# A grouped 3x3 convolution: one ring of twelve places for images and results, and a loop for the first eight images on TensorE

## The chip, the cores and the metric

The kernel runs on one core of a Trainium2 chip. A core has five engines that run their own instruction streams and meet at semaphores: TensorE (PE, matmuls; PEld is its weight load), VectorE (DVE), ScalarE (ACT), GpSimd (POOL) and SyncE (SP). Sixteen DMA engines move data between the memory of the chip (HBM) and the core's on-chip memory (SBUF). Matmul results land in PSUM, from where an engine has to copy them to SBUF before a DMA can store them. The metric is the time on the device in microseconds, the median over runs.

## What is computed

Sixteen images of 64 channels, 64 by 64, are convolved with a 3x3 kernel in 8 groups, with one row and column of zero padding; the result has 128 channels.

```python
batch, c_in, h, w, c_out, k, groups = 16, 64, 64, 64, 128, 3, 8
...
x_pad = np.pad(x, ((0, 0), (0, 0), (pad, pad), (pad, pad)), mode='constant')
for g in range(groups):
    for b in range(batch):
        for co in range(c_out_per_group):
            for ci in range(c_in_per_group):
                for kh in range(k):
                    for kw in range(k):
                        output[b, g * c_out_per_group + co] += \
                            weight[g * c_out_per_group + co, ci, kh, kw] * \
                            x_pad[b, g * c_in_per_group + ci, kh:kh+h, kw:kw+w]
```

Input and output are fp32. An image is 1 MB in HBM, a result 2 MB.

## The kernel before

**Layout.** `xx` holds NX = 8 images in bf16. For each image it has four quadrants of 32 partitions, of which three are used: the middle kernel row lies in the first quadrant (the image as loaded, 32 channels on the partitions, the two halves of the 64 channels side by side), the other two quadrants hold copies of it shifted by one row up and down. So a contraction over 96 partitions covers 32 channels times the three kernel rows, and the three kernel columns are three matmuls that add up in PSUM, on views of the image shifted by a column. `ob` is a list of NOB = 4 result buffers of 2 MB, `ps` two PSUM buffers, each for half an image (32 rows).

**The steps of an image n.** POOL issues its load, with a cast from fp32 to bf16 on the way (`load`, L133). VectorE makes the two shifted copies (`shifted`, L206, copies on L211), zero rows at the edges having been written once for all eight places at the start (L146). TensorE does each half image in 24 matmuls, for 3 kernel columns, 4 stripes of 8 rows and 2 halves of the channels, the two halves next to each other in the array (`matmuls`, L252, matmuls on L271). ScalarE copies each half from PSUM to the result buffer (`evacuate`, L284, copy on L291). SP issues the store (L298); image 0 is stored in two halves, and the store of the last image is issued at the very end (L63).

**What sets the order.** There is no scheduler: each engine's instructions stand in the order in which they are written, and `Order.wait` and `Order.done` put in the semaphores by hand. TensorE waits for the shifted copies (`ready`) and for the PSUM half being free (`free`, ScalarE's semaphore). ScalarE waits for the matmuls and, from image 4 on, for the store of image n-4 that used the same buffer (L286). The load of image n+8 waits on POOL for the matmuls of image n, which used the same place (L317). Before the last store is issued, all engines come to a barrier, and POOL clears the semaphores (L321).

**The start.** The first 36 rows of images 0 and 1 come in by one plain fp32 DMA on ScalarE's queue into the last result buffer (`raw`, L122), and are cast by ScalarE and VectorE (`cast`, L220); only the rest of these two images is loaded by POOL. The weights are loaded on SP's queue, spread out by VectorE (L189), transposed by TensorE (L196) and masked (L229). A small store of 64 KB to the result of the last image goes out early (L128); the first real store waits for it (`s_warm`). `spin` (L173) keeps TensorE busy with matmuls on zeros until the first image is ready, and `IDLE` puts in waits that pass at once on VectorE and ScalarE (L151).

Of the kernel before, what the change touches and what calls it, by code (L numbers as in the profile page):

```python
# [8 lines left out]
BF16 = mybir.dt.bfloat16  # L9
ALU = mybir.AluOpType  # L10

NX = 8
NOB = 4
KQ = (1, 0, 2)
ROWS = 36
SPINS = 11, 4, 4, 3, 3
IDLE = dict(ACT=90, DVE=40)


@with_exitstack  # L20
def kernel(
    ctx: ExitStack,
    tc: tile.TileContext,
    x: bass.AP,
    weight: bass.AP,
    groups: int,
    out: bass.AP,
):
    nc = tc.nc

    B, C, H, W = x.shape
    CO, CIg, K, _ = weight.shape
# [30 lines left out]
    last = nc.sync.dma_start(out[B - 1].rearrange("co h w -> co (h w)"), t["ob"][(B - 1) % NOB])  # L63
    tc.add_manual_dep(
        last.ins, section.name,
        mybir.DependencyInfo(mybir.DependencyClass.NoSync, mybir.DependencyReason.DATA), reason="order",
    )


class Order:  # L70
# [22 lines left out]
        return self.sem, self.n  # L93


def program(nc, x, weight, out, xx, ob, w_sb, wb, mask4, mask, ident, zero, wt, ps):
    H = W = 64
    HW, CIg, COg, R, NB = H * W, 8, 16, 8, 16
    sems = []
# [33 lines left out]
    def load(n):  # L133
        s, r0 = sem(f"ld{n}"), ROWS if n < 2 else 0
        nc.gpsimd.dma_start(  # L135
            xx[QC, n % NX, :, r0:, :].rearrange("c s h w -> c s (h w)"),
            x[n].rearrange("(s c) h w -> c s h w", s=2)[:, :, r0:, :].rearrange("c s h w -> c s (h w)"),
        ).then_inc(s, 16)
        landed[n] = (s, 16)
# [4 lines left out]
    edge = []  # L144
    for kh, row in ((0, 0), (2, H - 1)):
        e = DVE.done(nc.vector.memset(xx[quad(kh), :, :, row, :], 0.0))  # L146
# [22 lines left out]
    for n in range(2, NX):  # L169
# [31 lines left out]
    spin(2, (s_raw, 16))  # L201


    ready = {}

    def shifted(n, a, b, halves=slice(0, 2)):  # L206
# [28 lines left out]
    spin(3, w_ready)  # L235

    DVE.wait(d)
    spin(4, shifted(0, 0, 32, slice(1, 2)))
    DVE.wait(a)
    ready[0, 0] = shifted(0, 0, 32, slice(0, 1))  # L240
    for half in range(2):
        a = cast(ACT, nc.scalar.copy, 1, half)
    raw_read = [a, d]


    pe = nc.tensor
    stored = [nc.alloc_semaphore(f"st{i}") for i in range(NOB)]
    uses = [0] * NOB
    free = {0: w_ready}
    wrote = {}  # L250

    def matmuls(n, s):  # L252
        u = n % NX
        for kw in (1, 0, 2):
            w0, w1 = max(0, kw - 1), min(W, W + kw - 1)
            v0 = w0 - (kw - 1)
            ws = []
            for half in range(2):
                ws.append(wt[0:96, kw, 64 * half : 64 * half + 64])
            PE.wait(w_ready, e, ready[n, s])  # L260
            for c in range(4):
                if kw == 1 and c == 0:
                    PE.wait(free.get(s))
                for half in range(2):
                    pos = dict(tile_position=(0, 64 * half))
                    r0 = 32 * s + R * c
                    x_ap = xx[0:96, u, half, r0 : r0 + R, w0:w1]
                    o_ap = ps[s][:, 512 * c : 512 * c + 512].rearrange(
                        "p (h w) -> p h w", w=W
                    )[64 * half : 64 * half + 64, :, v0 : v0 + w1 - w0]  # L270
                    ins = pe.add_instruction(  # L271
                        mybir.InstMatmult(
                            name=nc.get_next_instruction_name(),
                            engine=mybir.EngineType.PE,
                            start_tensor_calc=kw == 1, stop_tensor_calc=kw == 2,
                            tile_size=(128, 64), ldweights=c == 0, **pos,
                            ins=[pe.lower_ap(x_ap, opt=False),
                                 pe.lower_ap(ws[half], opt=False, for_matmul_weights=True)],
                            outs=[pe.lower_ap(o_ap)],
                        )  # L280
                    )
        wrote[n, s] = PE.done(ins)

    def evacuate(n, s):  # L284
        slot = n % NOB
        if n >= NOB:  # L286
            ACT.wait((stored[slot], 16 * uses[slot]))
        elif n == NOB - 1:
            ACT.wait((s_warm, 16), *raw_read)
        ACT.wait(wrote[n, s])  # L290
        free[s] = ACT.done(nc.scalar.copy(ob[slot][:, 2048 * s : 2048 * s + 2048], ps[s]))  # L291
        if s == 1 or n == 0:
            o0 = 0 if n > 0 or s == 0 else HW // 2
            o1 = HW // 2 * (s + 1)
            SP.wait(free[s], (s_warm, 16))
            if n == NB - 1:
                return
            nc.sync.dma_start(outf[n][:, o0:o1], ob[slot][:, o0:o1]).then_inc(stored[slot], 16)  # L298
            uses[slot] += 1

    for n in range(NB):
        if n == 1:
            DVE.wait(raw_read[0])
            ready[n, 0] = shifted(n, 0, 32)
        DVE.wait(landed[n])
        if n < 2:
            ready[n, 1] = shifted(n, 32, 64)
        elif n == 2:
            ready[n, 0] = shifted(n, 0, 32)
            ready[n, 1] = shifted(n, 32, 64)  # L310
        else:
            ready[n, 0] = ready[n, 1] = shifted(n, 0, H)
        for s in range(2):
            matmuls(n, s)
# [8 lines left out]
    return [(stored[n % NOB], 16 * uses[n % NOB]) for n in range(NB, NB + NOB)]  # L323
# [1 line left out]
_INS = ['x', 'weight', 'groups']  # L325
_OUTS = [((16, 128, 64, 64), 'float32')]
# [30 lines left out]
```

## Time and profile before

| | us |
|---|---|
| median of 7 runs | 125.34 |
| lowest and highest | 125.18, 126.91 |
| the profiled execution, its own time | 126.12 |
| its span | 124.4 |
| PE, DVE, ACT, POOL busy in the span | 98.0, 77.3, 67.0, 15.4 |
| HBM read and written | 16.81 MB, 33.62 MB |
| one copy of a half image on ACT | 1.87 |
| one shifted copy of a whole image on DVE (two for each image) | 2.25 |
| first image matmul starts, last PSUM copy ends | 13.88, 111.12 |
| last store issued | 111.83 |

The profile is one execution of the program on the chip. Engine times are the time that its instructions ran; an engine that waits for a semaphore is idle. The DMA share is the mean busy share of the sixteen DMA engines; since the packets of an engine overlap a little at their ends, it can come out slightly above 1. Loads are counted by the bytes that they write, in bf16, which are half of those that they read, so a time with many loads shows fewer GB/s for the same busy engines. On the side of the instructions, "PEldq", "SPq" and the like name instructions that the engine's sequencer handles by itself: waits, branches, DMA issues.

The page's groups of the work on the images, with the number of instructions, then busy time and the mean of one in ns, then the idle time of the engine before them and what ended it:

```
L271 PE MATMUL ps<-xx,wt 96*64 96x504 bf16 (+1 forms) x768 | 88.7, 394 | 6.6 <-ACT ob L291 5.7
L291 ACT COPY ob<-ps 128x2048 f32<-128x2048 f32 x32 | 59.4, 1868 | 36.0 <-PE ps L271 21.0
L211 DVE COPY xx<-xx 32x8064 bf16<-32x8064 bf16 (+4 forms) x40 | 73.3, 1832 | 0.9
L135 POOL DMA_DIRECT2D xx<-in_x_dram x16 | 14.6, 914 | 49.0 <-PE ps L271 47.9
```

A matmul takes 394 ns from its start to its modelled end, but two run side by side and follow each other closely, so 768 of them fill 88.7 us.

### The profile page before, as it was taken

To read this page: it belongs to the slowest core of one execution; us is meant where nothing else is said; L and a number is where in the kernel's file an instruction comes from. 1 tells how busy PE (TensorE), PEld (TensorE's weight loads), DVE (VectorE), ACT (ScalarE), POOL (GpSimd) and SP (SyncE) were. 2 spreads that over 40 slices of the span, in tenths; PEclk is the share of its full clock that TensorE was granted. 3 is DMA by queue.
4 is the path that set the end of the run, shared out by engine and by line. 5 is a ranking of instruction groups with operands and counts; after the bars stand their busy time and mean duration, and the time that the engine had idled before them with its cause. 6 is when DMAs were issued, how large, how long until landed. Compare 5 with 4: busy or idle time off the path is not lost.

```text
span 124.4 us, 1320 instructions
## 1 busy us (share of the span) xinstructions
PE 98.0 (79%) x796; PEld 16.2 (13%) x220; DVE 77.3 (62%) x51; ACT 67.0 (54%) x36; POOL 15.4 (12%) x23
## 2 busy tenths in 40 slices
PE   5909999996999999569998984999999999910000
PEld 1203211110111111011010100111111111100000
DVE  4039999999999999999999999993000000000000
ACT  0049965777377665280565619077766777660000
POOL 5910001032030106310060000000000000000000
PEclk9995999999999999955899998599999999985555
DMA  4999999999999999999999999999999999999991
GB/s 63 340 225 206 213 215 208 261 292 329 335 313 382 319 348 316 361 335 316 332 429 414 313 385 432 432 432 427 437 427 421 427 437 432 432 427 432 437 395 58
DMA packets 4166, 42.72 MB, mean 343 GB/s; under 512 B 704, under 2 KB 832, under 8 KB 960
## 3 DMA queue, kind: packets, MB, share of 16 engines
q1 hardware_dynamic: 2736, 33.66, 64.2%
q0 software_dynamic: 1280, 7.80, 30.5%
q10 hardware_dynamic: 144, 1.18, 3.1%
q8 instruction: 4, 0.07, 0.2%
q14 instruction: 2, 0.02, 0.0%
HBM read 16.81 MB, written 33.62 MB: 405 GB/s over the span
## 4 chain that ended last, share of the span: by engine, by line
PE 39%; DMA 27%; DVE 17%; ACT 5%; issue 1%; SPq 0%
PE ps L271 39%; DMA out_dram<-ob 21%; DVE xx L211 16%; DMA w_sb<-in_weight_dram 6%; ACT ob L291 5%; DVE xx L220 1%; DVE wt L229 0%; DVE wb L189 0%; SPq L352 0%; SPq L50 0%
## 5 line engine op out<-in xcount | busy, mean ns | idle before, releaser
L271 PE MATMUL ps<-xx,wt 96*64 96x504 bf16 (+1 forms) x768 | 88.7, 394 | 6.6 <-ACT ob L291 5.7
L291 ACT COPY ob<-ps 128x2048 f32<-128x2048 f32 x32 | 59.4, 1868 | 36.0 <-PE ps L271 21.0
L211 DVE COPY xx<-xx 32x8064 bf16<-32x8064 bf16 (+4 forms) x40 | 73.3, 1832 | 0.9
L271 PEld LDWEIGHTS ps<-xx,wt 96*64 96x64 bf16 x192 | 12.8, 114 | 81.9 <-issue 59.3
L135 POOL DMA_DIRECT2D xx<-in_x_dram x16 | 14.6, 914 | 49.0 <-PE ps L271 47.9
L176 PE MATMUL ps<-zero 128*128 128x512 bf16 x25 | 9.0, 536 | 1.5 <-DVE mask L142 1.5
L220 ACT CAST xx<-ob 32x2304 bf16<-32x2304 f32 x3 | 6.3, 2109 | 0.1
L220 ACT ACT_TABLE_LOAD x1 | 1.3, 1283 | 8.1 <-DMA ob<-in_x_dram 8.1
L176 PEld LDWEIGHTS ps<-zero 128*128 128x128 bf16 x25 | 3.2, 133 | 6.4 <-issue 4.2
L189 DVE CAST wb<-w_sb 128x96 bf16<-128x96 f32 x3 | 0.6, 256 | 4.5 <-DMA w_sb<-in_weight_dram 4.5
L196 PE MATMUL ps<-ident,wb 128*96 128x128 bf16 x3 | 0.5, 311 | 3.1 <-DVE wb L189 3.1
L220 DVE CAST xx<-ob 32x2304 bf16<-32x2304 f32 x1 | 1.3, 1348 | 0.0
L146 DVE MEMSET xx<- 32x512 uint32 x2 | 1.0, 485 | 0.3 <-DVE xx L146 0.2
L141 DVE MEMSET zero<- 128x256 uint32 x1 | 0.3, 272 | 1.1 <-SPq L50 1.1
L196 PEld LDWEIGHTS ps<-ident,wb 128*96 128x96 bf16 x3 | 0.3, 184 | 3.6 <-issue 3.6
L183 DVE TENSOR_REDUCE mask<-mask 128x4 f32<-128x16 f32 x1 | 0.2, 179 | 0.8 <-POOL mask L165 0.8
L229 DVE TENSOR_TENSOR wt<-ps,mask 96x384 bf16<-96x384 f32 x1 | 0.6, 554 | 0.0
L160 POOL TENSOR_SCALAR_AFFINE_SELECT ident<-ident 128x128 bf16<-128x128 bf16 x1 | 0.3, 299 | 0.0
L155 POOL TENSOR_SCALAR_AFFINE_SELECT mask<-mask 128x16 f32<-128x16 f32 x1 | 0.2, 229 | 0.1
L165 POOL TENSOR_SCALAR_AFFINE_SELECT mask<-mask 128x16 f32<-128x16 f32 x1 | 0.2, 215 | 0.0
L338 POOL MEMSET const-float32-0.0<- 128x1 f32 x1 | 0.1, 100 | 0.3 <-issue 0.3
L143 DVE MEMSET ident<- 128x64 uint32 x1 | 0.1, 112 | 0.0
(4 smaller groups left out, 0.4 us busy)
## 6 DMA issues: line engine op xcount, KB each, us to landing
out_dram<-ob SPq DMA_DIRECT2D x15, 2048.0 KB, 17.0
xx<-in_x_dram POOLq DMA_DIRECT2D x14, 512.0 KB, 11.6
out_dram<-ob SPq DMA_DIRECT2D x2, 1024.0 KB, 13.1
ob<-in_x_dram ACTq DMA_DIRECT2D x1, 1152.0 KB, 7.0
xx<-in_x_dram POOLq DMA_DIRECT2D x2, 224.0 KB, 7.7
out_dram<-ob SPq DMA_DIRECT2D x1, 64.0 KB, 9.7
w_sb<-in_weight_dram SPq DMA_DIRECT2D x1, 36.0 KB, 7.3
```

What stands on the lines that cost most here:

```text
L135: nc.gpsimd.dma_start(xx[QC, n % NX, :, r0:, :].rearrange("c s h w -> c s (h w)"), x[n].rearrange("(s c) h w -> c s h w", s=2)[:, :, r0:, ...
L141: z = DVE.done(nc.vector.memset(zero, 0.0))
L146: e = DVE.done(nc.vector.memset(xx[quad(kh), :, :, row, :], 0.0))
L160: m4 = POOL.done(nc.gpsimd.affine_select(out=ident, in_=ident, compare_op=ALU.not_equal, fill=1.0, base=0, channel_multiplier=1, pattern=[ ...
L176: spun = nc.tensor.matmul(ps[1][:, 1536:2048], zero[:, 0:128], zero, start=True, stop=True)
L189: f = nc.vector.tensor_copy(wb[:, :, 32 * q : 32 * q + 32].rearrange("p t (g c) -> p t g c", c=CIg), wv[:, kh].rearrange("p c t -> p t c") ...
L196: ins = nc.tensor.matmul(ps[0][0:96, 128 * kw : 128 * kw + 128], wb[:, kw, :], ident, start=True, stop=True,)
L211: ins = nc.vector.tensor_copy(xx[quad(kh), u, halves, r0:r1, :].rearrange("c s h w -> c s (h w)"), xx[QC, u, halves, r0 + kh - 1 : r1 + kh ...
L220: return order.done(copy(xx[QC, n, half, 0:ROWS, :].rearrange("c h w -> c (h w)"), raw[32 * q : 32 * q + 32, 0 : ROWS * W],))
L229: w_ready = DVE.done(nc.vector.tensor_mul(wt.rearrange("p t (s g c) -> p (t s) g c", s=2, g=4), ps[0][0:96, 0:384].rearrange("p (t g c) -> ...
L271: ins = pe.add_instruction(mybir.InstMatmult(name=nc.get_next_instruction_name(), engine=mybir.EngineType.PE, start_tensor_calc=kw == 1, s ...
L291: free[s] = ACT.done(nc.scalar.copy(ob[slot][:, 2048 * s : 2048 * s + 2048], ps[s]))
```

## The change

**One ring.** `xx` has twelve places of 16 KB for each partition instead of eight, and the four result buffers are gone; together they take the same room. Image n lies in place n mod 12. Its result, in fp32, takes a whole place too: place (n + 8) mod 12. So the first four results lie in places 8 to 11, and the result of image n from 4 on overwrites image n-4. ScalarE no longer waits for a store. The load of image n+8 goes into the place of result n and waits on POOL for the store of that result, instead of for the matmuls of image n. As results now write over edge rows, VectorE zeroes the two edge rows of a place again for each image from 8 on, after its load has landed. There is one semaphore for each stored image; at the end ScalarE waits for fifteen of them.

**The loop.** Images 0 to 7 of TensorE are one loop of eight turns whose body holds the matmuls of one image. The address of the image is worked out from the loop's counter in registers; as built, the body has 48 matmuls, 32 register instructions, 4 semaphore instructions, a move, an add and a compare-and-branch. Images 8 to 15 stay written out with fixed addresses. Since a loop cannot wait for a different count each turn, the waits are now credits: VectorE adds one to `s_in` for each half that is ready, `s_out` counts free PSUM halves and starts at two, and TensorE takes one of each before a half. SP hands on ScalarE's "copied" as a credit to `s_out`, in its own order between the stores. The other engines get a branch at the place of the loop.

**One early column.** ScalarE copies one column of zeros into a new tile `first` at the start, before its idle waits. ScalarE's table of functions, which stood right before its first cast, is loaded there instead.

The core of the diff:

```diff
-NX = 8
-NOB = 4
+PLACES = 12
+AHEAD = 8
+LOOP = 8
...
-        xx=pool.tile([128, NX, 2, H, W], BF16, name="xx"),
-        ob=[pool.tile([128, H * W], FP32, name=f"ob{i}") for i in range(NOB)],
+        xx=pool.tile([128, PLACES, 2, H, W], BF16, name="xx"),
+        first=pool.tile([128, 1], FP32, name="first"),
...
+def result(xx, n):
+    return xx[:, (n + AHEAD) % PLACES].rearrange("p s h w -> p (s h w)").bitcast(FP32)
...
-    raw = ob[NOB - 1]
+    raw = result(xx, PLACES - AHEAD - 1)
...
+    def edges(places):
+        for kh, row in ((0, 0), (2, H - 1)):
+            ins = nc.vector.memset(xx[quad(kh), places, :, row, :], 0.0)
+        return DVE.done(ins)
+    e = edges(slice(0, AHEAD))
+    ACT.wait(z)
+    nc.scalar.copy(first, zero[:, 0:1])
...
+    s_in, s_out = sem("in"), sem("out")
+    nc.sync.sem_inc(s_out, 2)
...
+        if tell:
+            ins.then_inc(s_in, tell)
+            return None
...
-    def matmuls(n, s):
-        u = n % NX
+    def matmuls(u, s):
+        for taken in (s_in, s_out):
+            wait_then(pe, taken, 1, taken, "sem-sub-imm", 1)
...
-            PE.wait(w_ready, e, ready[n, s])
...
-                if kw == 1 and c == 0:
-                    PE.wait(free.get(s))
...
+    PE.wait(w_ready, e)
+    with pe.Fori(0, LOOP) as n:
+        for s in range(2):
+            matmuls(n % AHEAD, s)
+    for n in range(LOOP, NB):
+        for s in range(2):
+            matmuls(n % PLACES, s)
...
     def evacuate(n, s):
-        if n >= NOB:
-            ACT.wait((stored[slot], 16 * uses[slot]))
...
-        free[s] = ACT.done(nc.scalar.copy(ob[slot][:, 2048 * s : 2048 * s + 2048], ps[s]))
+        o = result(xx, n)
+        f = ACT.done(nc.scalar.copy(o[:, 2048 * s : 2048 * s + 2048], ps[s]))
+        wait_then(nc.sync, *f, s_out, "sem-add-imm", 1)
...
-            SP.wait(free[s], (s_warm, 16))
+            SP.wait((s_warm, 16))
...
         DVE.wait(landed[n])
+        if n >= AHEAD:
+            edges(slice(n % PLACES, n % PLACES + 1))
...
-        if n + NX < NB:
-            POOL.wait(wrote[n, 1])
-            load(n + NX)
+        if n + AHEAD < NB:
+            POOL.wait(stored[n])
+            load(n + AHEAD)
```

`wait_then(engine, s, value, then, mode, by)` is one semaphore instruction on an engine's own stream: it waits until `s` has reached `value`, and then changes `then` by `by`.

More of the change, by code (lines that the diff above doesn't have):

```diff
@@ L62 @@
             ))
-    last = nc.sync.dma_start(out[B - 1].rearrange("co h w -> co (h w)"), t["ob"][(B - 1) % NOB])
+    last = nc.sync.dma_start(out[B - 1].rearrange("co h w -> co (h w)"), result(t["xx"], B - 1))
     tc.add_manual_dep(
@@ L93, in done, with program @@
         return self.sem, self.n
-def program(nc, x, weight, out, xx, ob, w_sb, wb, mask4, mask, ident, zero, wt, ps):
+def program(nc, x, weight, out, xx, w_sb, wb, mask4, mask, ident, zero, first, wt, ps):
     H = W = 64
@@ L135, in load @@
         nc.gpsimd.dma_start(
-            xx[QC, n % NX, :, r0:, :].rearrange("c s h w -> c s (h w)"),
+            xx[QC, n % PLACES, :, r0:, :].rearrange("c s h w -> c s (h w)"),
             x[n].rearrange("(s c) h w -> c s h w", s=2)[:, :, r0:, :].rearrange("c s h w -> c s (h w)"),
@@ L143, in program @@
     m2 = DVE.done(nc.vector.memset(ident, 0.0))
-    edge = []
-    for kh, row in ((0, 0), (2, H - 1)):
-        e = DVE.done(nc.vector.memset(xx[quad(kh), :, :, row, :], 0.0))
+    def edges(places):
[5 more added lines that the diff above has]
+    nc.scalar.copy(first, zero[:, 0:1])
     for order, times in ((DVE, IDLE["DVE"]), (ACT, IDLE["ACT"])):
@@ L168, in program @@
     ))
-    for n in range(2, NX):
+    for n in range(2, AHEAD):
         load(n)
@@ L201, in program, with shifted @@
     spin(2, (s_raw, 16))
-    ready = {}
-    def shifted(n, a, b, halves=slice(0, 2)):
-        u = n % NX
+    s_in, s_out = sem("in"), sem("out")
+    nc.sync.sem_inc(s_out, 2)
+    def shifted(n, a, b, halves=slice(0, 2), tell=1):
+        u = n % PLACES
         lo, hi = max(a, 1), min(b, H - 1)
@@ L237, in program @@
     DVE.wait(d)
-    spin(4, shifted(0, 0, 32, slice(1, 2)))
+    spin(4, shifted(0, 0, 32, slice(1, 2), 0))
     DVE.wait(a)
-    ready[0, 0] = shifted(0, 0, 32, slice(0, 1))
+    shifted(0, 0, 32, slice(0, 1))
     for half in range(2):
@@ L246, in program, with wait_then @@
     pe = nc.tensor
[L247 to L250, printed above, removed]
-    def matmuls(n, s):
-        u = n % NX
+    stored = {}
+    p0 = PE.n
+    def wait_then(eng, s, value, then, mode, by):
+        eng.add_instruction(mybir.InstEventSemaphore(
+            name=nc.get_next_instruction_name(), engine=eng.engine,
+            sync_info=mybir.SyncInfo(
+                on_wait=[mybir.SyncWait(
+                    sync_type="semaphore", id=s.num, ant_name=s.name,
+                    wait_mode="sem-ge-imm", wait_value=value)],
+                on_update=[mybir.SyncUpdate(
+                    sync_type="semaphore", id=then.num, ant_name=then.name,
+                    update_mode=mode, update_value=by)],
+            ),
+        ))
+    def matmuls(u, s):
+        for taken in (s_in, s_out):
+            wait_then(pe, taken, 1, taken, "sem-sub-imm", 1)
         for kw in (1, 0, 2):
@@ L256, in matmuls @@
             v0 = w0 - (kw - 1)
-            ws = []
-            for half in range(2):
-                ws.append(wt[0:96, kw, 64 * half : 64 * half + 64])
-            PE.wait(w_ready, e, ready[n, s])
             for c in range(4):
-                if kw == 1 and c == 0:
-                    PE.wait(free.get(s))
                 for half in range(2):
@@ L267, in matmuls @@
                     x_ap = xx[0:96, u, half, r0 : r0 + R, w0:w1]
+                    w_ap = wt[0:96, kw, 64 * half : 64 * half + 64]
                     o_ap = ps[s][:, 512 * c : 512 * c + 512].rearrange(
@@ L277, in matmuls @@
                             ins=[pe.lower_ap(x_ap, opt=False),
-                                 pe.lower_ap(ws[half], opt=False, for_matmul_weights=True)],
+                                 pe.lower_ap(w_ap, opt=False, for_matmul_weights=True)],
                             outs=[pe.lower_ap(o_ap)],
@@ L281, in matmuls, with wrote @@
                     )
-        wrote[n, s] = PE.done(ins)
+        ins.then_inc(PE.sem, 1)
+    PE.wait(w_ready, e)
[5 more added lines that the diff above has]
+            matmuls(n % PLACES, s)
+    def wrote(n, s):
+        return PE.sem, p0 + 2 * n + s + 1
     def evacuate(n, s):
-        slot = n % NOB
-        if n >= NOB:
-            ACT.wait((stored[slot], 16 * uses[slot]))
-        elif n == NOB - 1:
+        if n == PLACES - AHEAD - 1:
             ACT.wait((s_warm, 16), *raw_read)
-        ACT.wait(wrote[n, s])
-        free[s] = ACT.done(nc.scalar.copy(ob[slot][:, 2048 * s : 2048 * s + 2048], ps[s]))
+        ACT.wait(wrote(n, s))
+        o = result(xx, n)
+        f = ACT.done(nc.scalar.copy(o[:, 2048 * s : 2048 * s + 2048], ps[s]))
+        wait_then(nc.sync, *f, s_out, "sem-add-imm", 1)
+        SP.seen[f[0].num] = f[1]
         if s == 1 or n == 0:
@@ L294, in evacuate @@
             o1 = HW // 2 * (s + 1)
-            SP.wait(free[s], (s_warm, 16))
+            SP.wait((s_warm, 16))
             if n == NB - 1:
                 return
-            nc.sync.dma_start(outf[n][:, o0:o1], ob[slot][:, o0:o1]).then_inc(stored[slot], 16)
-            uses[slot] += 1
+            if n not in stored:
+                stored[n] = nc.alloc_semaphore(f"st{n}"), 0
+            st, value = stored[n]
+            nc.sync.dma_start(outf[n][:, o0:o1], o[:, o0:o1]).then_inc(st, 16)
+            stored[n] = st, value + 16
     for n in range(NB):
@@ L303, in program @@
             DVE.wait(raw_read[0])
-            ready[n, 0] = shifted(n, 0, 32)
+            shifted(n, 0, 32)
         DVE.wait(landed[n])
+        if n >= AHEAD:
+            edges(slice(n % PLACES, n % PLACES + 1))
         if n < 2:
-            ready[n, 1] = shifted(n, 32, 64)
+            shifted(n, 32, 64)
         elif n == 2:
-            ready[n, 0] = shifted(n, 0, 32)
-            ready[n, 1] = shifted(n, 32, 64)
+            shifted(n, 0, 32)
+            shifted(n, 32, 64)
         else:
-            ready[n, 0] = ready[n, 1] = shifted(n, 0, H)
+            shifted(n, 0, H, tell=2)
         for s in range(2):
-            matmuls(n, s)
             evacuate(n, s)
-        if n + NX < NB:
-            POOL.wait(wrote[n, 1])
-            load(n + NX)
+        if n + AHEAD < NB:
+            POOL.wait(stored[n])
+            load(n + AHEAD)
     POOL.wait(SP.done(nc.sync.nop()))
     nc.clear_and_free_semaphores(sems)
-    return [(stored[n % NOB], 16 * uses[n % NOB]) for n in range(NB, NB + NOB)]
+    return [stored[n] for n in range(NB - 1)]
 _INS = ['x', 'weight', 'groups']
```

## The prediction

> **What bounds the kernel now.** I read the queue table first, then busy time in windows, then the waits, then the rows of small TensorE instructions. The queue table says what the 16 DMA engines spent their time on, as shares of the span:
>
> ```profile
> q1 hardware_dynamic: 2736, 33.66, 64.2%
> q0 software_dynamic: 1280, 7.80, 30.5%
> q10 hardware_dynamic: 144, 1.18, 3.1%
> q8 instruction: 4, 0.07, 0.2%
> ```
>
> Stores (q1), loads (q0), the first raw load (q10) and instruction fetches (q8) add up to 98% of 124.4 us. The windows (columns: PE, PEld, DVE, ACT, POOL busy, granted clock, DMA share, GB/s) show that nothing is left over in between:
>
> ```profile
> 6.00:18.00 12.00, 8.94 (x55) 2.53 (x27) 9.45 (x13) 8.91 (x5) 0.59 (x2) 0.86 1.06 217
> ...
> 24.00:30.00 6.00, 5.63 (x54) 0.68 (x12) 5.94 (x4) 4.07 (x3) 1.41 (x2) 1.00 1.03 315
> 30.00:60.00 30.00, 26.89 (x222) 3.51 (x56) 29.70 (x14) 16.37 (x9) 6.16 (x5) 0.89 1.02 332
> 60.00:75.00 15.00, 13.08 (x118) 1.94 (x28) 14.85 (x8) 8.07 (x5) 2.11 (x1) 1.00 1.02 382
> 75.00:120.00 45.00, 32.99 (x288) 5.27 (x72) 9.98 (x5) 25.25 (x14) 0.00 (x0) 0.86 1.01 430
> ```
>
> The DMA share is at or above 1 in every stretch from 6 to 120 us (packets overlap a little, hence 1.02). The GB/s rise only because a load is counted by its bf16 side. Only the last microseconds ramp down:
>
> ```profile
> 120.00:121.00 1.00, 0.00 (x0) 0.00 (x0) 0.00 (x0) 0.00 (x0) 0.00 (x0) 0.50 0.88 377
> 121.00:122.00 1.00, 0.00 (x0) 0.00 (x0) 0.00 (x0) 0.00 (x0) 0.00 (x0) 0.50 0.50 213
> 122.00:123.00 1.00, 0.00 (x0) 0.00 (x0) 0.00 (x0) 0.00 (x0) 0.00 (x0) 0.50 0.12 49
> ```
>
> So the kernel ends when the DMA engines have moved everything; the waits of the compute engines on stores are the symptom and cost nothing by themselves:
>
> ```profile
> ACT ob L291 <- PE ps L271: 21.0, 24, 2.9
> ...
> ACT ob L291 <- DMA out_dram<-ob: 15.1, 4, 4.9
> ```
>
> Consequence: an edit can only win in the ramp at the end (0.88+0.50+0.12 = 1.5 us of work spread over 3 us, so at most about 1.5 us), and can only lose by leaving the DMA engines without work.
>
> **Unit prices.** q1: 64.2% of 124.4 = 79.9 us for 33.66 MB, so 4.98 us for a 2.10 MB store and 2.49 for a half. q0: 37.9 us for 7.80 MB, so 2.55 us for a full load and 1.11 for each of the two short ones. q10: 3.9 us. One fetch: 0.2% x 16 x 124.4 / 4 = 1.0 us on one DMA engine. TensorE: 48 matmuls in 5.19 us, 2.59 for a half image (the ACT copies of the chain start 2.59 apart, 16.70, 19.29, 21.89).
>
> **Part 1: one ring, loads after stores.** Evacuations no longer wait for stores (15.1 us of ACT waits, 4 of them, go); what is late next is again the DMA, so this gains nothing. Loads 8 to 15 wait for the store of image n-8 instead of its matmuls. In the run of before, load 8 was issued at 19.55 and filled the time around 27 us; now the queue holds until then only the raw load, loads 0 to 7 and store 0: 3.9 + 6 x 2.55 + 2 x 1.11 + 4.98 = 26.4 us, at the share of 1.04 from 2.2 on: empty at 2.2 + 25.4 = 27.6. Store 1 is issued when ACT ends image 1 (24.48 + 1.87 = 26.35); the raw load took about 1.0 us from its issue (0.98) to a busy DMA, so store 1 starts at about 27.4. That just fits, with nothing to spare. Each delay of TensorE in its first four halves counts in full; with d us per half the hole is about 4d, plus 0.2 for TensorE's start through two waits of 51 ns and a register instruction. With 0.5 us of doubt either way I book +0.3 at d = 0. Later images need 4.98 + 2.55 = 7.5 us of DMA against 5.2 of TensorE, so the hole does not recur while d stays under 1.1.
>
> At the far end: before store 7 lands the queues must move about 3.9 + 17.5 + 8 x 4.98 + 7 x 2.55 = 79 us of work, at 1.02 from 2.2: 80 us. Load 15 lands some 8 us later (its 2.55 shared with store 8, an issue on POOL of up to 2.20, two trips of about 1), VectorE takes 2 x 2.25, TensorE 5.2, ACT 1.9: about 100 us. The last store must be queued when the others are through, at 117. 17 us of cover; a hole under d = 1 does not use it up.
>
> **Part 2: the loop.** Built, the loop holds 48 matmuls, 32 register instructions, 4 waits that take a credit, a move, an add and a compare-and-branch per image; nothing else on TensorE is longer than before, and the unrolled half keeps fixed addresses. The trace has no register instruction on TensorE. Its nearest rows (name, count, ns least/median/most):
>
> ```profile
> L87 PEldq EVENT_SEMAPHORE  x18: 51/51/51, 9.0 to 103.4; - x18
> ...
> L352 PEldq COMPARE_BRANCH  x1: 168/168/168, 0.9 to 0.9; - x1
> ```
>
> So a register instruction R lies between nothing (it runs ahead while the array works) and 168 ns; a matmul whose address comes from a register, M, between nothing and 51. Sequencer time of a half image: 16R + 24M + 2 x 51 + 168/2. At R = M = 51 it is 2.23 us, under the 2.59 of the array: hidden, d = 0. I take that, as TensorE's own control row is nearest in kind. At R = 110 (midway) and M = 51 it is 3.17, d = 0.58, hole 2.3. At R = 168 it is 4.10: TensorE slower than the DMA.
>
> The page "TensorE: Matmul & The Clock Gate" of the Trainium skill (Step-by-step) gives about 62 ns for a matmul that the sequencer decodes in software instead of hardware; no run here shows whether a register address forces that. By it, an estimate: 24 x 62 = 1.49 us, which with R = 51 makes 2.49, just hidden.
>
> The loop also shortens the instruction stream: 796 matmuls + 220 weight loads + some 20 others = 1036 for 4 fetches, about 259 each; now 56 + 99 + 512 = 667, so 2 or 3 fetches. Each one less takes 1.0 us off one DMA engine. It helps only if that engine is among the last of the ramp: between 0 and 1.0, booked at -0.3. The body of 99 instructions, begun about 60 into the stream, should sit inside one block.
>
> Against the loop speaks the page "Runtime: NRT & Kernel Launch" (Instruction fetch mechanics): a taken branch to a page out of the window stalls for a fetch. The row here is a fetch of 1.0 us. If every back edge paid it, the one back edge before store 1 would add 1.0 us to the hole; I leave that out of the sum, since the body should not leave its block.
>
> **Part 3: ACT's early column.** It pulls the table load (1.28 us, ended 9.33) off the path of ACT's first cast. That cast ended at 9.35 + 2.11 = 11.46; VectorE came to it at about 12.30 after an unbroken row from 8.31 (waiting for weights). VectorE sets TensorE's start: gain 0.
>
> **Part 4: small changes.** SP now relays each freed half to TensorE: one wait of 17 ns and a signal each, say 0.1 us; ACT stands idle 0.67 to 0.78 us a half for TensorE, which hides it. Queued behind these waits on SP are the stores (0.33 us to issue), and the wait for the warm-up store, over at 17.74, before the first copy ends at 18.57; without that cover TensorE's third half would slip. VectorE: 16 small memsets, by the 72 and 112 ns of its small ones 0.2 us an image on 4.5, under TensorE's 5.2. POOL's clearing of semaphores grows from 2 to 9 pairs (0.18 us each: +1.2 us) before the last store may go out; covered by the 17 us above, otherwise 1.2. ACT's 15 closing waits instead of 4, at 17 ns, lie beside the last stores.
>
> **Sum.** 124.4 + 0.3 - 0.3 + 0.1 = 124.5. The profiled execution took 126.12 with that span, the median is 125.34, so I carry differences over: about 125.5.
>
> **The rivals.** About 1% (1.25 us) is what a measurement can tell from no change.
>
> A, the loop is hidden (0.50): 124.5 to 126.5, the ends being the fetch gain of 1.0 and a hole of 1.2.
>
> B, slower: the sequencer decides, one mechanism at one place, the hole at 27 us before store 1. It is felt by over 1% from d = 0.33 on (4 x 0.33 + 0.3 - 0.3), which is R of about 94 ns. At R = 110 +2.3: 127.7; range 126.6 to 129.5. For it: everything small on TensorE costs three times SP's 17 ns, so 51 may be the least of a three-step register instruction. Against: TensorE's 18 waits of 51 ns leave the halves of before 2.59 apart, so small instructions do run ahead of the array. 0.34.
>
> C, R near 168 (0.10): TensorE gives an image every 8.2 us, under the DMA's pace. Image 7 is out at 14 + 16 x 4.10 + 1.9 = 81.5; then 9 stores and 2 loads remain, (44.8 + 5.1)/1.02 = 49: end of DMA at 132, +9 us: 134.
>
> D, faster by over 1% (0.06): both dropped fetches sat on the engines that end last, and no hole opens: -1.3 to -1.5, 123.9.
>
> So: 125.5 predicted; own range of A 124.5 to 126.5. For 8 in 10 the range takes in B: 124.4 to 129.5, leaving out C, D and a little more of B (about 0.2). Faster 0.06, same 0.50, slower 0.44.
>
> **What would show it.** A: TensorE's evacuations in images 0 to 7 still 2.59 us apart, DMA share at least 1.0 in 27 to 30, fewer instruction packets, last copy near 100 us, no ACT wait on stores. B: copies 2.9 to 3.6 apart and a DMA share under 0.8 in one stretch near 28. C: shares under 1 until 80. I am wrong if the DMA share falls anywhere else, if the last store is issued after 117, or if a packet takes longer than now.

## The result and the profile after

| | before | after |
|---|---|---|
| median of the runs, us | 125.67 (61 runs) | 127.19 (24 runs) |
| lowest and highest | 125.04, 126.91 | 125.56, 128.18 |
| the profiled execution, its own time | 126.12 | 127.09 |
| its span | 124.4 | 125.0 |
| time less span | 1.7 | 2.1 |

The ratio of the compared runs is **1.0074, 95% interval 1.0053 to 1.0095**: slower, by 0.7% in the compared executions. The comparison leaves out executions over 1.5% above the fastest of their kernel (8 of the 26 of after, profiled ones included, and none of before), so the ratio is smaller than the quotient of the two medians (1.012); the granted clocks of the 8 (0.885 to 0.908) overlap those of the others (0.888 to 0.925).

The queue table of the page after (columns: packets, MB, share of 16 engines' span) is to be read against that of before:

```profile
q1 hardware_dynamic: 2736, 33.66, 63.7%
q0 software_dynamic: 1280, 7.80, 31.0%
q10 hardware_dynamic: 144, 1.18, 3.0%
q8 instruction: 2, 0.03, 0.1%
```

Stores: 63.7% of 125.0 = 79.6 us, as before (79.9). Fetches: 2 instead of 4. But the loads, with the same 1280 packets and the same bytes, took 31.0% of 125.0 = 38.8 us of each DMA engine instead of 30.5% of 124.4 = 37.9. That is +0.8 us by these rounded shares and +0.7 by the packet records themselves (38.69 against 38.00), a little more than the 0.6 by which the span grew.

The busy times by window of the kernel after (columns as in the prediction; the last two are DMA share and GB/s) say where. A packet is counted whole in the window in which it starts, so short windows have to be read together with their neighbours:

```profile
24.00:30.00 6.00, 5.74 (x54) 1.18 (x12) 5.94 (x4) 3.96 (x3) 0.22 (x1) 1.00 1.03 433
30.00:60.00 30.00, 29.36 (x271) 6.94 (x69) 29.35 (x20) 20.70 (x12) 5.67 (x5) 1.00 1.01 345
60.00:75.00 15.00, 15.00 (x142) 3.90 (x36) 11.35 (x10) 10.79 (x6) 1.75 (x2) 1.00 1.02 359
75.00:120.00 45.00, 25.33 (x218) 4.97 (x52) 15.29 (x13) 18.65 (x10) 1.56 (x2) 0.80 1.01 407
...
33.00:34.00 1.00, 1.00 (x13) 0.28 (x3) 1.00 (x1) 0.31 (x1) 0.00 (x0) 1.00 1.20 246
34.00:35.00 1.00, 1.00 (x13) 0.35 (x4) 0.97 (x2) 1.00 (x1) 0.26 (x1) 1.00 0.85 123
35.00:36.00 1.00, 1.00 (x12) 0.14 (x3) 1.00 (x1) 0.55 (x1) 1.00 (x1) 1.00 1.09 197
36.00:37.00 1.00, 1.00 (x12) 0.22 (x3) 1.00 (x1) 0.80 (x1) 1.00 (x1) 1.00 0.83 221
37.00:38.00 1.00, 1.00 (x13) 0.22 (x2) 0.99 (x2) 1.00 (x1) 0.13 (x1) 1.00 1.01 418
```

The long windows look as full as before: no share under 1.0. The short ones show one stretch, 34 to 36 us, with the engines counted as busy (0.85 and 1.09) but moving 123 and 197 GB/s. Bytes of loads count half, so a stretch of loads alone is expected to be low, but not that low: between 6 and 18 us, nearly all loads, the kernel after moves 217 GB/s. In before the same microseconds hold a store beside a load:

```profile
34.00:35.00 1.00, 1.00 (x12) 0.11 (x2) 1.00 (x1) 1.00 (x1) 0.00 (x0) 1.00 1.09 336
35.00:36.00 1.00, 1.00 (x14) 0.11 (x2) 0.97 (x2) 0.35 (x2) 0.00 (x0) 1.00 1.06 336
```

The packet records of the trace name the transfer. Load 8, the first that waits for a store, was issued at 29.78 and its packets run from 33 to 37 us: they start as store 1 drains, and the first packet of store 2 (issued 31.74) comes only at 35.65. They took 852 ns on the mean. Every later load of this execution has 624 to 627 ns, and so has load 8 in before. That is (852 - 624) x 64 packets / 16 engines = 0.9 us per engine: **busy engines, but slower packets**.

The waits of the kernel after (engine, line, what was waited for: us, times, longest) show what the change took away and what it put in:

```profile
POOL xx L142 <- DMA out_dram<-xx: 66.0, 8, 23.2
ACT xx L325 <- PE ps L296: 31.4, 32, 5.6
```

ScalarE waits for TensorE only; its waits on stores are gone. POOL, with nothing else to do, now waits for stores before it issues a load.

### The profile page after: what moved, and what is told of

Same layout as the page of the kernel before. It is cut to its first block, busy times and chain, and to the rows that moved or that the text cites. A ratio compares the mean times of both kernels' runs of the same rounds, so it can differ in the third digit from the quotient of the medians.

```text
span 125.0 us, 1710 instructions
## 1 busy us (share of the span) xinstructions
PE 95.5 (76%) x796; PEld 22.8 (18%) x220; DVE 79.0 (63%) x67; ACT 67.5 (54%) x37; POOL 14.3 (11%) x23
## 3 DMA queue, kind: packets, MB, share of 16 engines
q1 hardware_dynamic: 2736, 33.66, 63.7%
q0 software_dynamic: 1280, 7.80, 31.0%
HBM read 16.81 MB, written 33.62 MB: 403 GB/s over the span
## 5 line engine op out<-in xcount | busy, mean ns | idle before, releaser
L296 PE MATMUL ps<-xx,wt 96*64 (+2 forms) x768 | 85.6, 385 | 3.9 <-PEq L269 3.9
L325 ACT COPY xx<-ps 128x2048 f32<-128x2048 f32 x32 | 59.7, 1865 | 31.4 <-PE ps L296 31.4
L296 PEld LDWEIGHTS ps<-xx,wt 96*64 96x64 bf16 x192 | 19.4, 111 | 69.5 <-issue 69.1
L142 POOL DMA_DIRECT2D xx<-in_x_dram x16 | 13.5, 850 | 67.1 <-DMA out_dram<-xx 66.0
L189 PE MATMUL ps<-zero 128*128 128x512 bf16 x25 | 9.7, 571 | 1.5 <-DVE mask L149 1.5
L154 DVE MEMSET xx<- 32x64 uint32 (+1 forms) x18 | 2.8, 153 | 10.4 <-DMA xx<-in_x_dram 9.4
L237 ACT CAST xx<-xx 32x2304 bf16<-32x2304 f32 x3 | 6.3, 2110 | 5.0 <-DMA xx<-in_x_dram 5.0
L237 DVE CAST xx<-xx 32x2304 bf16<-32x2304 f32 x1 | 1.3, 1348 | 0.0
```

What stands on the lines that cost most here:

```text
L142: nc.gpsimd.dma_start(xx[QC, n % PLACES, :, r0:, :].rearrange("c s h w -> c s (h w)"), x[n].rearrange("(s c) h w -> c s h w", s=2)[:, :, r ...
L154: ins = nc.vector.memset(xx[quad(kh), places, :, row, :], 0.0)
L237: return order.done(copy(xx[QC, n, half, 0:ROWS, :].rearrange("c h w -> c (h w)"), raw[32 * q : 32 * q + 32, 0 : ROWS * W],))
L296: ins = pe.add_instruction(mybir.InstMatmult(name=nc.get_next_instruction_name(), engine=mybir.EngineType.PE, start_tensor_calc=kw == 1, s ...
L325: f = ACT.done(nc.scalar.copy(o[:, 2048 * s : 2048 * s + 2048], ps[s]))
```

## The experiments

"Span" below is the median over the timed executions that enter the comparison, "outside" the median of time less span. "Slow load packets" is from the one profiled execution: the load packets after 22 us that took over 700 ns, their time above 624 ns, summed and divided by 16 engines; "slow store packets" is the same for the 16 KB packets of the stores, above their usual 611 ns.

| kernel | ratio to before, 95% interval | span, us | outside, us | slow load packets, us | slow store packets, us |
|---|---|---|---|---|---|
| before | 1 | 123.7 to 123.8 | 1.73 | 0.06 | 0.05 |
| after | 1.0074 [1.0053, 1.0095] | 124.6 | 2.08 | 0.94 | 0.03 |
| no_loop | 1.0067 [1.0035, 1.0100] | 124.5 | 2.02 | 0.73 | 0.11 |
| loads_after_stores | 1.0041 [1.0011, 1.0072] | 124.5 | 1.71 | 0.72 | 0.22 |
| loop_old_buffers | 1.0038 [1.0016, 1.0060] | 123.9 | 2.09 | 0.04 | 0.05 |
| ahead_10 | 0.9998 [0.9974, 1.0022] | 123.7 | 1.83 | 0.01 | 0.02 |
| one_store_later | 1.0123 [1.0072, 1.0175] | 125.0 | 2.12 | 1.09 | 0.32 |
| sems_together | 1.0065 [1.0029, 1.0101] | 124.6 | 1.83 | 0.22 | 0.14 |
| slow_loop | 1.0270 [1.0218, 1.0323] | 126.8 | 2.01 | 0.63 | 0.99 |
| ahead_10_sems | 0.9993 [0.9971, 1.0015] | 123.7 | 1.80 | 0.01 | 0.02 |
| store_2_in_halves | 1.0057 [1.0032, 1.0081] | 124.2 | 2.11 | 0.13 | 0.80 |
| ahead_9 | 1.0013 [0.9991, 1.0034] | 123.7 | 1.83 | 0.02 | 0.05 |
| no_early_column | 1.0089 [1.0059, 1.0119] | 124.6 | 2.10 | 0.54 | 0.14 |
| whole_first_store | 0.9998 [0.9977, 1.0020] | 123.9 | 1.84 | 0.18 | 0.22 |

**no_loop**: the kernel after, all sixteen images of TensorE written out.

```diff
-LOOP = 8
+LOOP = 0
```

> The changed kernel with images 0 to 7 written out instead of looped (same credits, same ring). Theory 1 (the loss comes from the loads that follow the stores, which leave load 8 alone in the queues at 33 to 37 us): the same slow load 8, ratio to before 1.005 to 1.013, that is no faster than the changed kernel's 1.0074, and two more instruction fetches (4 packets). Rival 2 (the loop's register instructions cost it): ratio back to 0.997 to 1.002. Rival 3 (one tile for images and results costs it): as theory 1.

Ratio 1.0067, its interval lying over that of after. The loop is not the cause, and the four fetches that come back cost nothing that shows.

**loads_after_stores**: the kernel before, with this one part of the change.

```diff
-            POOL.wait(wrote[n, 1])
+            POOL.wait((stored[n % NOB], 16 * uses[n % NOB]))
```

> The kernel before with one line changed: the load of image n+8 waits for the store of image n instead of its matmuls. Theory 1: ratio 1.004 to 1.010, a load 8 with packets well over 624 ns, last DMA packet 0.5 to 0.9 us later. Rivals 2 and 3: ratio 0.998 to 1.002, since neither the loop nor the shared tile is in it.

Ratio 1.0041, and 0.7 us more span than before. Its slow load is load 9, nearly alone from 40 to 42 us, with 768 ns a packet (load 8, the one that was expected to be slow, has 650); the window of this kernel, in the columns from above:

```profile
40.00:42.00 2.00, 2.00 (x22) 0.24 (x6) 1.99 (x2) 1.33 (x2) 0.00 (x0) 1.00 1.02 188
```

Share 1.02, 188 GB/s: the same sign in a kernel that has neither ring, loop nor early column.

**loop_old_buffers**: the complement, the kernel after with eight image places and four result buffers, loads after the matmuls; loop, credits and early column stay.

```diff
-PLACES = 12
+PLACES = 8
+NOB = 4
...
+        if n >= NOB:
+            ACT.wait(stored[n - NOB])
...
-            POOL.wait(stored[n])
+            POOL.wait(wrote(n, 1))
```

> The changed kernel with the buffers of before: eight places for images, four result buffers, loads after the matmuls, copies from image 4 on wait for the store of n-4; the loop, the credits and the early column stay. Theory 1: ratio 0.994 to 1.001, a little under 1 by the two fetches saved. Rival 2: 1.005 to 1.010. Rival 3: as theory 1.

The ratio of 1.0038 missed the expectation. But the span is back within 0.2 us of before and the slow packets are gone (this run takes out the ring together with the waits on stores; loads_after_stores has the waits alone); what remains is outside the span, 2.09 against 1.73. So the loss has two parts, which the next runs take one by one.

**ahead_10**: ten images are loaded ahead instead of eight; load n+10 waits for store n.

```diff
-AHEAD = 8
+AHEAD = 10
```

> The changed kernel with ten loads issued at the start instead of eight (results then begin in place 10; loads 10 to 15 follow stores 0 to 5). Theory 1: the queues hold 5.1 us more work when load 8 would have been alone, so the loss goes: ratio 0.994 to 1.002, no load with packets well over 640 ns after 30 us. Rivals 2 and 3: stays at 1.005 to 1.010.

Ratio 0.9998, span as before, no slow packets. Loads still follow stores, but by the time that the first of them moves there are two loads more behind the first stores.

**one_store_later**: load n+7 waits for store n, so each load comes a store later.

```diff
-        if n + AHEAD < NB:
+        if 1 <= n and n - 1 + AHEAD < NB:
             POOL.wait(stored[n])
-            load(n + AHEAD)
+            load(n - 1 + AHEAD)
```

> The changed kernel with each late load waiting for one store more: load n+7 for the store of image n, so load 8 for store 1. Theory 1a (load 8 is slow because it runs alone between store 1 and store 2, 852 ns a packet instead of 624): it now meets stores 2 and 3, its packets return to under 660 ns, span 0.5 to 0.9 us under the changed kernel's 125.0, ratio 1.000 to 1.004. Theory 1b (the queues simply hold too little work near 30 us): the hole grows, since store 2 was issued at 31.7 and store 1 was through at 33; ratio 1.008 to 1.020.

It was meant to move load 8 away from the gap between two stores, and did not: load 8 fell into the next gap, after store 2, at 38 us with 858 ns a packet. The window:

```profile
38.00:40.00 2.00, 2.00 (x22) 0.65 (x6) 1.97 (x2) 1.49 (x1) 0.75 (x1) 1.00 1.02 156
```

So it did not separate the two theories: the ratio of 1.0123 lies in the range of 1b, but load 8 was alone and slow again. It shows the same sign at another time, and the loss grows with fewer loads ahead.

**sems_together**: the kernel after, with the fifteen store semaphores taken in one row before the first load, so that they don't alternate with those of the loads. POOL then clears 2 ranges of semaphores instead of 9.

```diff
+    store_sems = [nc.alloc_semaphore(f"st{i}") for i in range(NB - 1)]
...
-                stored[n] = nc.alloc_semaphore(f"st{n}"), 0
+                stored[n] = store_sems[n], 0
```

> The changed kernel with the fifteen store semaphores allocated in one row, so that POOL clears 2 ranges at the end instead of 9. The time lies 2.07 us above the span in the changed kernel and 1.72 above it before. Theory (the 9 ranges make this difference): time minus span 1.70 to 1.78, ratio 1.003 to 1.006 instead of 1.0074, span as in the changed kernel. Rival (the early column or the loop makes it): time minus span stays at 2.0 to 2.1.

Outside the span 1.83 instead of 2.08: that part of the loss is 0.25 us, though the 1.70 to 1.78 that were expected were not reached. The ratio, 1.0065, just misses its range too and hardly moved, since the executions' spans lie between 123.5 and 125.4 and hide it. The profiled execution was one of the shortest (123.5); in it load 8 was alone just as in after, but its packets took 658 ns. So a load alone is not always slow.

**slow_loop**: a test of the second rival. Seven more waits, all passed long ago, in each half of the loop.

```diff
+        for _ in range(extra):
+            wait_then(pe, s_w, 16, s_slow, "sem-add-imm", 1)
...
-            matmuls(n % AHEAD, s)
+            matmuls(n % AHEAD, s, 7)
```

> The changed kernel with seven extra semaphore waits of TensorE in each half image of the loop, about 150 ns each in its stream: sequencer time of a half from about 2.3 to 3.3 us. By the prediction's hole of 4d before store 1 (d = 0.7): copies of images 0 to 7 about 3.3 us apart, one stretch near 30 us with a DMA share under 0.8, span +2 to +3.5 us over the changed kernel. Rival (the price is smaller, other cover is left): +0 to +1.

The timeline of ScalarE (start, length, line, operation, idle before) in slow_loop:

```profile
17.14 1.87 ACT L328 COPY xx<-ps 128x2048 f32<-128x2048 f32 x1 [2.67 <-PE ps L299]
20.31 1.87 ACT L328 COPY xx<-ps 128x2048 f32<-128x2048 f32 x1 [1.31 <-PE ps L299]
23.99 1.87 ACT L328 COPY xx<-ps 128x2048 f32<-128x2048 f32 x1 [1.81 <-PE ps L299]
27.18 1.87 ACT L328 COPY xx<-ps 128x2048 f32<-128x2048 f32 x1 [1.32 <-PE ps L299]
```

and its windows:

```profile
28.00:29.00 1.00, 1.00 (x10) 0.22 (x3) 0.99 (x2) 1.00 (x1) 0.00 (x0) 1.00 0.53 221
29.00:30.00 1.00, 1.00 (x13) 0.21 (x2) 1.00 (x1) 0.04 (x1) 0.00 (x0) 1.00 0.21 90
```

The fourth copy starts at 27.18, in after at 24.59: d = 0.65 us for each half. The share falls to 0.53 and 0.21 at the place that the prediction named, and nowhere else as low; the span is 2.2 us longer than that of after, where 4d + 0.2 gives 2.8. But the hole itself is only 0.47 + 0.79 = 1.3 us. Behind it, from 33.7 to 34.9 us, 27 packets of a store, at the end of that store and with no other transfer running, take 1071 ns on the mean instead of 611; in all, slow store packets cost 0.99 us here and 0.03 in after.

**ahead_10_sems**: both remedies together.

```diff
-AHEAD = 8
+AHEAD = 10
...
+    store_sems = [nc.alloc_semaphore(f"st{i}") for i in range(NB - 1)]
```

> Ten loads at the start and the store semaphores in one row, together: both repairs on the changed kernel. If they add, ratio 0.996 to 0.999 (ahead_10 had 0.9998 with 1.82 us outside the span, 0.1 to go there). Rival: the 1.82 stays, ratio 0.999 to 1.001.

Ratio 0.9993: the change is at the time of before, not below it. The time outside the span stays at 1.80, as the rival said, so the two remedies do not add up.

**store_2_in_halves**: the kernel after, with company for load 8.

```diff
-        if s == 1 or n == 0:
-            o0 = 0 if n > 0 or s == 0 else HW // 2
+        if s == 1 or n in (0, 2):
+            o0 = 0 if n not in (0, 2) or s == 0 else HW // 2
```

> The kernel after, but image 2 is stored in two halves, as image 0 is, so that a store stands in the queues beside load 8 at 33 us (in the kernel after, load 8 has them to itself there: its packets take 852 ns on the mean, against 624 in the kernel before). [...] Theory (a load that is alone in the queues moves slowly, and that is the loss): load 8's packets under 700 ns, no stretch under 200 GB/s between 33 and 36 us, ratio to the kernel before 1.000 to 1.005. Rival (the loss is that DMA work is queued late everywhere, whichever load is beside which store): ratio 1.005 to 1.010 as the kernel after.

Load 8's packets are at 637 ns, as expected. The ratio of 1.0057 is not: it lies just above the one expectation and inside the other. The span is 0.4 us under that of after and 0.5 over that of before. The windows show what came instead:

```profile
32.00:33.00 1.00, 1.00 (x12) 0.35 (x4) 0.99 (x2) 0.28 (x1) 0.00 (x0) 1.00 1.36 377
33.00:34.00 1.00, 1.00 (x13) 0.23 (x3) 1.00 (x1) 0.60 (x1) 0.00 (x0) 1.00 0.64 139
34.00:35.00 1.00, 1.00 (x13) 0.22 (x2) 0.97 (x2) 1.00 (x1) 0.08 (x1) 1.00 1.16 295
```

The 0.64 at 33 is no hole: with the 1.36 before it, it makes two full microseconds, and again few GB/s. By the packet records, 20 of the last packets of store 1, from 31.9 to 33.1 us, take 1083 ns on the mean and up to 1281, instead of 611; no other transfer has packets running there. Slow packets of loads and stores together come to 0.13 + 0.80 = 0.93 us, against 0.94 + 0.03 = 0.97 in after. So company for load 8 did not remove the slow packets; they moved to the end of store 1, which now was alone.

**ahead_9**: one load more ahead.

```diff
-AHEAD = 8
+AHEAD = 9
```

> The kernel after with AHEAD = 9: nine images are loaded before any store, so load n+9 waits for store n. Theory (the loss is the first load after the first stores, alone in the queues): load 9 is now the one that waits for store 0 and meets the same gap between stores 1 and 2; but load 8 lies beside store 0. If that same gap remains the ratio is 1.004 to 1.008; if one load more in the queues fills it, 0.998 to 1.003. With AHEAD = 10 the ratio was 0.9998. 8 ranges of semaphores to clear outside the span, so time minus span about 2.0.

Ratio 1.0013, span as before. One load more is enough. Its window over the bad stretch:

```profile
33.00:38.00 5.00, 5.00 (x50) 1.01 (x10) 4.96 (x3) 3.73 (x2) 2.20 (x2) 1.00 1.00 429
```

Full, and only stores. Outside the span it has 1.83, not the 2.0 that was expected: see the last section.

**no_early_column**: the kernel after without the early copy.

```diff
-    ACT.wait(z)
-    nc.scalar.copy(first, zero[:, 0:1])
```

> The kernel after without ScalarE's early copy of one column. Theory (VectorE sets TensorE's start, the early column brings nothing): ratio to the kernel before 1.005 to 1.010, within 0.3% of the kernel after, first ACT copy of a result within 0.3 us of 16.81. Rival (it does save a table load on the path): first ACT copy later by 0.5 to 1.3 us and ratio above 1.010. Time minus span: 2.0 if the early column has nothing to do with the 0.1 us that the ranges of semaphores leave unexplained, 1.95 if it has.

Ratio 1.0089, the interval lying over that of after. In its profile ScalarE's table load takes 1.28 us right before the first cast again, and the first result copy starts at 16.02, against 16.81 in after; the raw load that the casts wait for landed 0.8 us earlier in that execution (7.05 against 7.83). So the first copy missed its expectation, within 0.3 us of 16.81, by coming earlier, and the ratio gained nothing from it. The column brings nothing, and has no part in the time outside the span (2.10).

**whole_first_store**: a try at beating both, ahead_10_sems with image 0 stored in one piece and fewer store semaphores for ScalarE to wait on at the end.

```diff
-        if s == 1 or n == 0:
-            o0 = 0 if n > 0 or s == 0 else HW // 2
-            o1 = HW // 2 * (s + 1)
+        if s == 1:
...
-            nc.sync.dma_start(outf[n][:, o0:o1], o[:, o0:o1]).then_inc(st, 16)
+            st = store_sems[min(n, NB - AHEAD)]
+            nc.sync.dma_start(outf[n], o).then_inc(st, 16)
```

> The kernel after with AHEAD = 10 and the store semaphores in one row (ahead_10_sems: ratio 0.9993), and two edits more that its cover allows: image 0 is stored in one piece instead of two halves, and the stores of images 6 to 14 count on one shared semaphore, so that ScalarE closes with 7 waits instead of 15. Theory (the DMA engines' work sets the span, and with two loads more ahead no store is needed early): the two halves took 5.1 us of the DMA engines in their packets, a whole store 4.9, so the span falls by about 0.2 us; time minus span goes from 1.80 to 1.72 to 1.78; ratio to the kernel before 0.996 to 0.999. Rival (a store is needed early, or the end ramp takes what is saved): 0.999 to 1.002.

Ratio 0.9998: missed. The full-size packets of all its stores took 78.9 us per engine; in after those and the halves of image 0 take 73.8 + 5.2 = 79.0. There was nothing to save: the first store's packets, amid loads, took 637 ns instead of the 611 to 620 of later ones.

## Why the prediction was right, and where it was not

The forecast was 125.5, 124.4 to 129.5, most likely within 1%. The median of 127.19 lies inside, but 0.7 us above rival A's own range of 124.5 to 126.5, though A's mechanism, the hidden loop, is the one that held. It lies in the range of rival B (126.6 to 129.5), whose slow loop did not happen. The ratio of the compared executions, 1.0074 on 125.34, makes 126.3, inside A's range. What slowed the kernel stood in none of the rivals; that the stated range holds the upper median as well is luck, by room that was left for something else.

- **The loop is hidden: right, with wrong sizes that made up for each other.** The step was 2.23 us of sequencer time under 2.59. The row of the loop's register instructions in the trace of after (ns least/median/most, first and last start):

```profile
L296 PEldq FUSED_REGOPS  x256: 46/46/46, 13.8 to 55.6; - x128
```

  R is 46 ns, where 51 was taken, and the copies of the first eight images start 2.59 apart, up to small fractions (16.81, 19.40, 21.99, 24.59, 27.18). no_loop confirms it. slow_loop shows the stream itself, since there the array waits for the sequencer. By its instruction records, the part of a half with 16 register instructions, 24 matmuls and 6 weight loads takes 1.84 us (16R + 24M was forecast as 2.04), a wait 0.151 us from start to start (0.051 forecast), and the end of the loop 0.46 us for an image (0.17 forecast). From these, an estimate for a half in after: 1.84 + 2 x 0.151 + 0.46/2 = 2.37 us. It is hidden with 0.22 us to spare, not 0.36.

  What a matmul with a register address costs, M, was not measured by itself. If each register instruction takes 46 ns of the 1.84 us, at most (1.84 - 0.74)/24 = 46 ns are left for a matmul, an estimate, where the forecast took 51. The Trainium skill's page "TensorE: Matmul & The Clock Gate" (Step-by-step) has about 62 ns for a software decode. By it, an estimate, 24 x 62 ns = 1.49 us on top of the 0.74 would be 2.22, more than the 1.84 of slow_loop; so unless the two overlap, that price does not show here.
- **"It just fits, with nothing to spare": right.** Store 1's first packets run at 28.1, directly behind the last half of store 0. The 0.3 us that were booked for a hole were not needed.
- **The price of a slower loop (rival B): right in place, near in size.** It did not happen in the change itself; slow_loop made it happen, at 28 to 30 us. The size is near in part by luck: the hole is 1.3 us where 4d + 0.2 gives 2.8, and slow store packets behind it, which the forecast did not have, cost 0.99.
- **"Can only lose by leaving the DMA engines without work": this step failed.** So did the unit price that goes with it, 2.55 us for every load. The sum of the first part had only one way to lose, a hole at 27 us, and put +0.3 on it. In after the share stays up, yet the loads' packets take 0.7 us longer. The prediction named this only as a sign that it was wrong ("if a packet takes longer than now"), without a price.
- **What causes that: the load n+8 waiting for store n.** Put into before by itself, it costs 0.7 us of span; taken out of after together with the ring, all but 0.2 of the 0.9 go; with nine or ten loads ahead, all go. That is shown. That the time is lost in slow packets, of a transfer that has the queues to itself or nearly so, is seen in the profiles: loads in after, no_loop, loads_after_stores, one_store_later and no_early_column, ends of stores in store_2_in_halves and slow_loop. Loads and stores together, the slow packets come to 0.68 us and more in all these, and to 0.11 or less in the kernels whose span is that of before, except whole_first_store, which has 0.40. Being alone is not enough: sems_together ran through the same gap once with load 8 at 658 ns, and in after store 1 was alone from 29 to 33 us, at 613 ns on the mean. **Why the packets slow down stays open.**
- **Carrying differences of the span over to the time: failed by 0.35 us.** The step assumed that what lies around the span is constant, at 1.7; it is 2.1. Of that, 0.25 us go when the store semaphores stand in one row. The prediction had POOL's longer clearing (nine pairs, now from 105.4 to 106.9) covered, and inside the span it is.
- **Fetches, -0.3: not seen.** They fell from 4 to 2, as expected, but no_loop with 4 has the same span as after to 0.1 us, and loop_old_buffers with 2 the same as before to 0.2 us.
- **The early column, 0: right** (no_early_column).
- **The far end: mis-sized, without effect.** The last copy starts at 103.4 instead of ending at about 100, and the last store is issued at 107.0: 10 us ahead of the 117, not 17.
- **The sum.** In spans, 124.5 - 124.4 = +0.1 was predicted. Measured is 124.6 against 123.7 to 123.8, so +0.8 to 0.9, plus 0.35 outside; the ratio's interval makes it 0.7 to 1.2 us in all, for the compared executions.

## What to carry to other kernels

In a kernel bound by its DMA engines, a full DMA share is not enough: read the GB/s beside it, against a stretch with the same kind of transfer, for busy engines can move less. When a load is put behind the completion of a store, count what is still queued at that moment; here the span with eight loads ahead of the first store was 0.9 us longer, and with nine no longer than before. When an edit cures one slow transfer and the time stays, look at the packets of its neighbours before calling the cause refuted: in store_2_in_halves they had slowed instead. And look at the time outside the span for both kernels before carrying a span's difference over.

## What was not expected of the hardware

- The packets of one transfer of the same shape differ by a third from case to case: load 8 at 852 (after), 797 (no_loop) and 858 ns (one_store_later) where it was alone in the queues, 658 ns in another execution where it was alone too (sems_together), 624 beside stores. The ends of stores do the same: 1083 ns in store_2_in_halves and 1071 in slow_loop against the usual 611. Single packets reach 1874 ns. The spans of all timed executions of after spread over 123.5 to 126.1 us, those of ahead_10_sems over 123.4 to 124.1.
- The time outside the span moves in steps. It is 2.01 to 2.12 us for every kernel in which POOL clears 9 ranges of semaphores, 1.80 to 1.84 with 8, 7 or 2 ranges in the changed kernels, and 1.71 to 1.73 in the two with the old code and 2 ranges. A price for each range would have given ahead_9, with 8, about 2.0; it has 1.83. The step between 8 and 9 is measured but its cause isn't known, and neither is that of the last 0.1: whole_first_store, with 7 closing waits on ScalarE instead of 15, still has 1.84.
- On TensorE, register instructions take 46 ns each, a semaphore instruction 51 (151 from start to start in slow_loop, where nine stand in a row), and the loop's compare-and-branch 76 to 227, median 208; all of it, together with the weight loads and matmuls of a half, stays hidden in after behind 2.59 us of the array.
